# A two-layer decoder trunk: first output products split ahead of the last values' emptying, memory rows stored from GpSimd's queue, initial query slabs crosswise

## The chip, the core and the metric

The kernel runs on one core of a Trainium2 chip. Its engines work side by side, each with its own instruction stream in order: TensorE (PE) multiplies matrices from SBUF into the banks of PSUM; VectorE (DVE) and ScalarE (ACT) read PSUM and SBUF and write SBUF; GpSimd (POOL) works on SBUF alone; SyncE (SP) issues DMA transfers, and POOL's stream can issue them too. An instruction waits on semaphores for what it reads and for the buffers that it writes. The metric is device time in microseconds (us) of one execution.

## The reference

The input is x (1 x 1024 x 1024) with 256 memory tokens. Two layers, each `x <- LayerNorm(alpha * x + W_out [main * silu(g_main) ; mem * silu(g_mem)])`, with all of u_main, q_mem and the two gates from one projection `h = x @ w_in` (3072 columns).

- Layer 0's main branch is a causal pooling over windows of 2, 4, 8 and 16 tokens with a linear map per group.
- After layer 0, `x @ w_kv_shared` gives keys, values (16 heads of 64) and forget-gate logits.
- Layer 1's main branch is causal attention with a forgetting bias:

```python
logits = jnp.einsum('bqhd,bkhd->bhqk', qi, k) * scale
logits = logits + (ci[..., :, None] - cum_k[:, :, None, :])
p = jax.nn.softmax(jnp.where(mask[None, None], logits, -jnp.inf), axis=-1)
return jnp.einsum('bhqk,bkhd->bqhd', p, v)
```

- In both layers the memory branch is a 4-head attention (heads of 128) from q_mem into the 256 memory tokens, whose keys and values come from `mem @ w_mem_kv`.

## The kernel before, in words

**Numbers.** Products run at a precision near float32 with two or three matmuls for one. A tensor is held in parts: a rounded high part, a low part (the difference) and, for the three-term kind, a second rounding called top. ACT makes the high and top parts with casts, DVE the low part with a subtraction (`hi_lo`, lines 195 to 200; `scaled_hi_lo` for the two-half kind in layer 1; `gp_` variants on POOL). `three` lists the pairs of parts to be multiplied.

**Buffers.** Tiles come from pools by tag, each tag with a fixed number of buffers: "w" (6) holds split weights, "raw" (4) weights as they land, "T" (6) transposed probabilities and inputs of the output product, "V" (4) in layer 1 the memory rows and, after them, the attention's values; in PSUM "pj" (2 banks), "L" (3), "T" (2) and "O" (1). A new tile waits for the last use of the buffer that it takes.

**Order.** A planner orders each engine's instructions by their place in the program and by when it expects their inputs. Inside `with tc.manual_schedule(engines={PE})` PE keeps the program's order. `tc.keep_in_program_order(ins)` (often `pin`) keeps one instruction behind the one that was written before it for the same engine. DMA issues are instructions of SP or POOL like others, and a DMA that waits holds up what stands behind it in its queue.

**A slab** (`slab`, line 325) is one 128-column strip of a projection, over all 1024 tokens: in layer 1, for n in the two halves of the tokens and pc in the two halves of the depth, 12 matmuls of 512 columns, 48 in all. Each n has its own PSUM bank, and is emptied by the function that was passed in, right after its 24th matmul. It is a generator that yields at each matmul, so slabs can be pumped in pieces between other work.

**Layer 1's memory attention** (`mem_attention`, line 461). The norm of layer 0 (`norm`, line 668) writes the new stream X in rows of 128 tokens: normalised by DVE, split, and transposed into X by DMA (line 695). Meanwhile PE projects the four heads' memory keys (`keys`, line 419, 24 matmuls of 256 columns each, into "pj"), which need no X. Then, head by head, one query slab over X (line 470, into "pj", emptied by `q_split`, lines 457 to 459) and the head's memory values (`vals`, line 422, 24 matmuls). Here the planner orders PE too. Logits, softmax and values follow, with gate slabs between them. Last, DVE multiplies each head's rows by its gate (line 541) and SP stores them to the DRAM tensor `y1d` (line 542).

**Into the forgetting attention.** `v_first` (line 855) projects the first two pairs' values: for each of 8 token tiles 24 matmuls of 272 columns into "pj", emptied by ACT (line 872) and DVE (lines 873, 874) into two "V" buffers. `fox` (line 1150) then goes through 16 heads of 8 query tiles with the program's own order on PE, pumping projection slabs between the heads' products, `LAG` = 6 tiles ahead of the products with the values (`values`, line 1100).

**The drain.** After the last head, six more steps (hd = 16) bring the values of the last tiles. PE's filler is `OutProj.early` (line 604): the output product of layer 1 for the first 256 tokens with the third quarter of its depth, the memory rows. In the last step come the values of tiles 0 to 3 of head 15, emptied by ACT (line 1124) and DVE (1125), gated by POOL (1134) and stored by SP (1136). Then `OutProj.rest` (line 615) takes the other products in the order of line 619: (0, 0) is tokens 0 to 255 with the first third of the depth, whose rows were stored long before. It loads them (634), splits them in two halves on ACT and DVE, pinned (lines 637 to 643), and multiplies (599), then goes on with 256 tokens at a time, and normalises and stores each group.

Of the kernel before, what the change touches and what calls it, by code (L numbers as in the profile page):

```python
# [9 lines left out]
F32 = mybir.dt.float32  # L10
# [4 lines left out]
AF = mybir.ActivationFunctionType  # L15
# [3 lines left out]
P = 128  # L19
# [6 lines left out]
MH = 4  # L26
# [46 lines left out]
def run(units):  # L73
    for _ in units:
        pass
# [3 lines left out]
def trunk_kernel(ctx, tc, x, xT, memT, win, wk, wv0, wv, wmk, wmv, wout, poolw, pscale, lng, lnb, bforget, out):  # L79
# [33 lines left out]
    def T(shape=(P, S), dt=F32R):  # L113
        return sb(list(shape), "T", 6, dt)
# [338 lines left out]
    def q_split(l, to, acc):  # L453

        if not l:
            return hi_lo(to, acc)
        nc.scalar.activation(to.hi, acc, AF.Copy, scale=un1s[0])
        nc.vector.scalar_tensor_tensor(to.lo, acc, un1s[0], to.hi.bitcast(F32), ALU.mult, ALU.subtract)
        nc.scalar.activation(to.top, acc, AF.Copy, scale=un1s[0])

    def mem_attention(l, X, kv, qtile, ytile, yd, behind=None, before=None, last=None):

        (mk, v, undo), keys, vals = kv
        qs = []
        if l:
            for h in range(MH):
                keys(h)
        for h in range(MH):
            q = parts_of(qtile, [P, S])
            run(slab(win[l, 8 + h], X, lambda cols, acc: q_split(l, q[:, cols], acc)))  # L470
            qs.append(q)
            if not l:
                keys(h)
            vals(h)
        seeing[0] = None
        ys, gs = [ytile() for _ in range(MH)], [G() for _ in range(MH)]
        pt, fill = {}, Fill()
        for h in range(MH):
            fill.add(gate_units(win[l, 20 + h], gs[h], X), SLAB)
        if behind:  # L480
            fill.add(behind, 24 * NH)

        def probs(i):

            p, two = sb([P, MH, NMEM], "P", 4), sb([P, 2, MH, NMEM], "P", 4, F16)
            m, ms, sm, r = tiny(MH), tiny(MH), tiny(MH), tiny(MH)
            for hp in range(2):
                lg = ps([P, 2, NMEM], "L", 3)
                for n, j in ((0, 0), (0, 1), (1, 1), (2, 1), (1, 0), (2, 0)):
                    h = 2 * hp + j  # L490
                    a, b = three(qs[h][:, i * P : (i + 1) * P], mk[:, h, :])[n]
                    nc.tensor.matmul(lg[:, j, :], a, b, start=(n, j) == (0, 0), stop=(n, j) == (2, 0))
                pair = slice(2 * hp, 2 * hp + 2)
                nc.vector.tensor_reduce(m[:, pair], lg, AX.X, ALU.max, negate=True)
                nc.vector.tensor_scalar(ms[:, pair], m[:, pair], MSCALE, None, ALU.mult)
                for j in range(2):
                    h = 2 * hp + j
                    nc.scalar.activation(
                        p[:, h, :], lg[:, j, :], AF.Exp, bias=ms[:, h : h + 1], scale=MSCALE, accum_out=sm[:, h : h + 1],
                    )  # L500
            nc.vector.tensor_scalar(r, sm, 1.0 / PSCALE, None, ALU.mult)
            nc.vector.reciprocal(r, r)
            for h in range(MH):
                nc.scalar.activation(two[:, 0, h, :], p[:, h, :], AF.Copy, scale=r[:, h : h + 1])
                nc.vector.scalar_tensor_tensor(
                    two[:, 1, h, :], p[:, h, :], r[:, h : h + 1], two[:, 0, h, :], ALU.mult, ALU.subtract,
                )
            pt[i] = T([P, 2, MH, 2, P], F16)
            nc.sync.dma_start_transpose(
                pt[i].rearrange("p e h m q -> p (e h m) q"), two.rearrange("p e h t -> p (e h t)"),  # L510
            )

        def values(c, h):
            acc = ps([P, NH], *(("O", 1) if h == 1 else ("T", 2)))
            for j in range(4):
                t = pt[4 * c + j]
                mm3(acc[:, j * P : (j + 1) * P], [
                    (v[:, h, 2 * e + m, :], t[:, f, h, m, :])
                    for m in range(2) for e, f in ((0, 0), (0, 1), (1, 0))
                ])  # L520
            nc.vector.tensor_scalar(ys[h][:, c * NH : (c + 1) * NH], acc, undo[:, h : h + 1], None, ALU.mult)

        with tc.manual_schedule(engines={PE}):
            for t in range(ST + 2):
                part = fill.left / (ST + 2 - t)
                if t < ST:
                    probs(t)
                if before and t == ST - 2:
                    before()
                if last and t == ST:  # L530
                    last(0)
                at = {5: (0.3, 0, 0.1, 0.6), 9: (0.6, 0, 0.1, 0.3)}.get(t, (1, 0, 0, 0))
                for h in range(MH):
                    fill.pump(part * at[h])
                    if t in (5, 9):
                        values((t - 5) // 4, h)
            fill.pump(float("inf"))
        if last:
            last(1)
        for h in range(MH):  # L540
            nc.vector.tensor_tensor(ys[h], ys[h], gs[h], ALU.mult)  # L541
            nc.sync.dma_start(yd[:, h, :], ys[h])

    class OutProj:

# [2 lines left out]

        def __init__(self, l, wtile, yd):
            self.l, self.wtile, self.yd, self.ws, self.accs = l, wtile, yd, [{}, {}], None  # L550
            self.raws, self.n = [], 0

        def fetch_two(self, land):

# [49 lines left out]
        def early(self, y, ys):  # L604
# [7 lines left out]
            self.accs = self.open()  # L612
            yield from self.products(self.accs, 2, ys)

        def rest(self, resid, X, dst):
            order = [(sp, c) for sp in range(ST // 2) for c in (2, 0, 1)]
            accs, splits, gb = {}, [24], []
            if self.accs:
                accs[0], order[:6], splits = self.accs, [(0, 0), (1, 2), (0, 1), (1, 0), (1, 1)], [16, 24]
            if X is not None:  # L620
                self.split(splits.pop())

            def loads():

                for v in (lng, lnb):
                    t = sb([P, D], "P", 4)
                    nc.sync.dma_start(t, v[self.l].partition_broadcast(P))
                    gb.append(t)

            for sp, c in order:  # L630
                if c == 2:
                    accs[sp] = self.open((("T", 2), ("T", 2), ("L", 3), ("O", 1))) if 0 in accs and sp == 1 else self.open()
                src, ys = T([P, 4, 2 * P], F32), parts_of(T, [P, 4, 2 * P])
                nc.sync.dma_start(src, self.yd[c, :, :, sp * 2 * P : (sp + 1) * 2 * P])
                joins = bool(self.accs) and (sp, c) == (0, 0)
                if joins:
                    pin = tc.keep_in_program_order
                    tiles = [(ys[:, :, a * P : (a + 1) * P], src[:, :, a * P : (a + 1) * P]) for a in range(2)]
                    for to, y in tiles:
                        pin(nc.scalar.copy(to.hi, y))  # L640
                        pin(nc.vector.tensor_tensor(to.lo, y, to.hi.bitcast(F32), ALU.subtract))
                    for to, y in tiles:
                        pin(nc.scalar.copy(to.top, y))
                else:
                    hi_lo(ys, src)
                if splits:
                    self.split(splits.pop(0), X is None)
                if not gb and not splits:
                    loads()
                if c == 1:  # L650
                    zs = rows_of(resid, sp)
                run(self.products(accs[sp], c, ys, X is None and sp == ST // 2 - 1 and c == 1, joins or c > 0))
                if X is not None and (sp, c) == (0, 0):
                    scale_of_norm(gb)
                if X is not None and c == 0 and sp:
                    scales_of_weights(sp - 1)
                if X is not None and c == 0 and sp in (1, 2):
                    keep(sp - 1)
                if c == 1:
                    norm(sp, accs.pop(sp), gb, zs, X, dst)  # L660
# [152 lines left out]
    with tc.tile_pool(name="in1", bufs=1) as in1:  # L813
# [286 lines left out]
        def values(hd, c, o):  # L1100
# [20 lines left out]
                part(n == 0)  # L1121
            own, other = slice(64 * b, 64 * b + 64), slice(64 - 64 * b, P - 64 * b)
            oc = o[own, c * NH : (c + 1) * NH]
            nc.scalar.activation(oc, acc[other, :], AF.Copy, scale=un[own])  # L1124
            nc.vector.scalar_tensor_tensor(oc, acc[own, :], un[own], oc, ALU.mult, ALU.add)

        bfb = const.tile([P, HEADS], F32, name="bfb")
        nc.sync.dma_start(bfb, bforget.partition_broadcast(P))
# [21 lines left out]
        def fox(following, out_proj, head):  # L1150
# [8 lines left out]
            for hd in range(HEADS + 1):  # L1159
# [16 lines left out]
                for i in range(ST if hd < HEADS else LAG):  # L1176
# [50 lines left out]
                    fill.pump(part * FRAC[0])  # L1227
                    for what in split:
                        turn(*what)
                    older = past[0]  # L1230
                    if older and older[1] % 4 == 0:
                        values(older[0], older[1] // 4, older[2])
# [81 lines left out]
```

## Time and profile before

| what | value |
|---|---|
| three runs | 1187.91, 1190.2, 1191.57 us, median 1190.2 |
| the profiled execution | 1191.22 us, span 1189.5 us |
| granted clock of TensorE | 0.998 |
| PE, DVE, ACT, POOL busy | 98%, 66%, 58%, 24% of the span |
| HBM read, written | 116.01 MB, 22.61 MB |

The page of the profile shows one execution: the busy time of each engine; the span in 40 slices; the DMA queues; the chain of work that ended last; the costliest groups of instructions. Further views answer for one engine, tile or stretch: a timeline (start and busy time in us, engine, line, operation, what it writes and reads, how many; in brackets the idle time before it and what ended it) and waits (who waited for whom, in total, times, longest). "PEld" is the loading of weights, beside PE's matmuls, "SPq" an instruction in SP's queue. Names are the program's: `pj` is a PSUM bank, `w` a weight tile. Matmuls are pipelined and the ends of PE's rows are modelled, so the distance of starts tells more than the busy time of a short row.

### The profile page before, as it was taken

How to read it: one execution, taken by the hardware profiler on the slowest of the kernel's cores; microseconds unless marked ns; L12 is line 12 of the kernel's file. 1: busy time of each engine (PE TensorE's matmuls, PEld its weight loads, DVE VectorE, ACT ScalarE, POOL GpSimd, SP SyncE). 2: the span in 40 equal slices, each digit the busy share in tenths (PEclk: the TensorE clock that was granted, in tenths of full speed). 3: DMA queues.
4: the chain of work that ended last, by engine and by line, in shares of the span. 5: the costliest groups of instructions: out<-in, count | busy, mean ns of one | idle time of the engine just before them, and what ended most of it. 6: DMA issues, size and time to landing. Idle time of an engine off the chain costs nothing. (4 is left out here: it accounts for less than half of the span.)

```text
span 1189.5 us, 19847 instructions
## 1 busy us (share of the span) xinstructions
PE 1166.9 (98%) x6941; PEld 672.4 (57%) x6941; DVE 781.3 (66%) x1841; ACT 684.7 (58%) x1514; POOL 285.8 (24%) x437
## 2 busy tenths in 40 slices
PE   9999999999999999999999999999999999999996
PEld 5566766555555557556664555555555545455553
DVE  6744675555765557457645888778877788875554
ACT  6577875875563234467422776667766767674210
POOL 4322001310000000000002454555545444750000
PEclk9999999999999999999999999999999999999999
DMA  7575656854375555355734889989996999984430
GB/s 262 179 257 185 165 103 208 250 176 150 97 266 170 149 156 134 110 142 108 196 126 115 180 188 208 201 168 194 208 204 146 167 198 205 216 202 161 167 106 35
DMA packets 286196, 203.89 MB, mean 171 GB/s; under 512 B 224912, under 2 KB 238352, under 8 KB 286096
## 3 DMA queue, kind: packets, MB, share of 16 engines
q1 hardware_dynamic: 279696, 181.59, 61.4%
q0 software_dynamic: 6400, 21.04, 5.5%
q8 instruction: 54, 0.88, 0.3%
q14 instruction: 46, 0.38, 0.1%
HBM read 116.01 MB, written 22.61 MB: 117 GB/s over the span
## 5 line engine op out<-in xcount | busy, mean ns | idle before, releaser
L359 PE MATMUL pj<-A,w 128*128 128x512 f16 (+2 forms) x2896 | 662.3, 382 | 1.7 <-ACT w L198 0.7
L359 PEld LDWEIGHTS <-w 128*128 128x128 f16 (+1 forms) x2560 | 245.7, 98 | 278.4 <-issue 9.6
L1053 ACT ACTIVATE T<-MK,s 128x512 f32<-128x512 f32 x192 | 111.1, 579 | 66.3 <-DVE s L1045 49.4
L1082 DVE SCALAR_TENSOR_TENSOR P<-T,s,P 128x512 f16<-128x512 f32 x192 | 112.0, 613 | 39.2 <-ACT P L1081 38.1
L1081 ACT ACTIVATE P<-T,s 128x512 f16<-128x512 f32 x192 | 103.1, 576 | 53.1 <-issue 28.9
L599 PEld LDWEIGHTS <-T 128*128 128x128 bf16 x736 | 70.5, 98 | 87.9 <-issue 3.9
L1019 POOL TENSOR_SCALAR_AFFINE_SELECT raw<-R 128x256 f32<-128x256 f32 (+3 forms) x128 | 59.9, 470 | 180.7 <-DVE s L1045 97.7
L323 PE MATMUL L<-A 128*128 128x512 f16 (+3 forms) x384 | 84.7, 326 | 5.5 <-DVE s L1045 5.4
L199 DVE TENSOR_TENSOR w<-raw,w 128x512 bf16<-128x512 f32 x74 | 51.9, 701 | 54.9 <-ACT w L198 39.3
L902 POOL MEMSET G<- 128x128 f32 x1 | 0.2, 204 | 334.1 <-DVE V L541 334.1
L359 PEld LDWEIGHTS pj<-A,w 128*128 128x128 f32 x352 | 65.3, 188 | 16.2 <-ACT w L198 1.1
L199 DVE TENSOR_TENSOR T<-T,T 128x1024 bf16<-128x1024 f32 x22 | 26.8, 1220 | 65.5 <-PE pj L599 43.4
L323 PEld LDWEIGHTS <-A 128*128 128x128 f16 x384 | 37.3, 98 | 48.8 <-issue 7.6
L178 POOL TENSOR_TENSOR w<-B,w 128x512 f16<-128x512 f32 x54 | 62.9, 1166 | 4.0
L198 ACT CAST w<-raw 128x512 fp32r<-128x512 f32 x76 | 46.7, 615 | 25.0 <-DMA raw<-in_win_dram 11.2
L1107 PEld LDWEIGHTS <-V 128*64 128x64 f16 (+1 forms) x1152 | 50.6, 104 | 13.3 <-issue 5.6
L1107 PE MATMUL O<-T,V 128*64 128x128 f16 (+1 forms) x1152 | 57.5, 220 | 0.4 <-ACT T L1053 0.4
L198 ACT CAST T<-T 128x1024 fp32r<-128x1024 f32 x22 | 23.1, 1048 | 55.6 <-DMA T<-y0d 24.7
L599 PE MATMUL pj<-B,T 128*128 128x512 bf16 (+1 forms) x192 | 53.1, 385 | 0.4 <-DVE G L676 0.4
L1045 DVE CUSTOM_DVE_ANT_0 MK<-L,R,scales 128x512 f32<-128x512 f32 x64 | 45.3, 708 | 9.7 <-PE L L323 9.3
L200 ACT CAST w<-raw 128x512 bf16<-128x512 f32 x78 | 48.2, 618 | 3.3 <-PE pj L359 1.9
L599 PE MATMUL L<-B,T 128*128 128x512 bf16 (+1 forms) x168 | 47.3, 394 | 0.4 <-ACT T L640 0.4
(292 smaller groups left out, 1851.0 us busy)
## 6 DMA issues: line engine op xcount, KB each, us to landing
raw<-in_win_dram SPq DMA_DIRECT2D x66, 256.0 KB, 3.4
W<-in_win_dram POOLq DMA_DIRECT2D x48, 256.0 KB, 4.1
R<-cumd SPq DMA_DIRECT2D x16, 512.0 KB, 4.5
B<-in_win_dram SPq DMA_DIRECT2D x15, 512.0 KB, 4.8
y0d<-Y SPq DMA_DIRECT2D x12, 512.0 KB, 4.4
raw<-in_wout_dram SPq DMA_DIRECT2D x24, 256.0 KB, 2.8
T<-y0d SPq DMA_DIRECT2D x12, 512.0 KB, 4.6
A<-A SPq DMA_DIRECT2D x24, 256.0 KB, 4.0
```

Of the source, the lines that this page charges most:

```text
L178: pin(nc.gpsimd.tensor_tensor(to.lo, src, to.hi, ALU.subtract))
L198: pin(nc.scalar.copy(to.hi, src))
L199: pin(nc.vector.tensor_tensor(to.lo, src, to.hi.bitcast(F32), ALU.subtract))
L200: pin((top or nc.scalar.copy)(to.top, src))
L323: nc.tensor.matmul(acc, a, b, start=i == 0, stop=i == len(terms) - 1)
L359: nc.tensor.matmul(accs[n], a[:, k, :], b[:, pc * 4 + k, n * NH : (n + 1) * NH], start=seen[n] == 1, stop=seen[n] == 3 * KT,)
L599: nc.tensor.matmul(accs[a][nh], y, w, start=kt == 8 and i == 0, stop=kt == 7 and i == 2,)
L1019: tc.keep_in_program_order(nc.gpsimd.affine_select(C[:, :w], R[:, lo:up], [[-1, w]], ALU.is_ge, -NEG, base=w - P, channel_multiplier=1,))
L1053: nc.scalar.activation(e, p[:, lo:up], AF.Exp, bias=top, scale=-1.0, accum_out=sums[:, n, hd % 2, i : i + 1],)
L1081: nc.scalar.activation(pair[:, lo:up], e, AF.Copy, scale=r)
L1082: nc.vector.scalar_tensor_tensor(pair[:, L + lo : L + up], e, r, pair[:, lo:up], ALU.mult, ALU.subtract)
L1107: nc.tensor.matmul(acc[rows, (i % 4) * P : (i % 4) * P + P], v[:, b, 2 * j : 2 * j + (1 if e else 2), :].rearrange("p e d -> p (e d)"), pt ...
```

## The change

Three parts.

1. In layer 1's memory attention the query slabs of heads 0 and 1 are issued crosswise, with the program's order on PE: 24 matmuls (the first half of the tokens) of head 0, 24 of head 1, the rest of head 0, the values of head 0, the rest of head 1, the values of head 1. Head 0's slab takes its banks from "L" in place of "pj". Heads 2 and 3 stay as they were.
2. In layer 1 the four stores of the memory rows to `y1d` are issued from POOL's queue, pinned there, in place of SP's. Layer 0 keeps SP.
3. The load and the split of the first quarter of the output product, (0, 0), move from `rest` to a new function `begin`, which `fox` calls in the last step of the drain, ahead of the last values. The two instructions that empty these values (only those of the last head's first half) are now pinned, and so stand behind the split on ACT and DVE. The matmuls on that quarter stay in `rest`.

```diff
+        def queries(h, banks=("pj", 2)):
             q = parts_of(qtile, [P, S])
-            run(slab(win[l, 8 + h], X, lambda cols, acc: q_split(l, q[:, cols], acc)))
             qs.append(q)
+            return slab(win[l, 8 + h], X, lambda cols, acc: q_split(l, q[:, cols], acc), banks)
+
+        if l:
+            with tc.manual_schedule(engines={PE}):
+                one, two = queries(0, ("L", 3)), queries(1)
+                run(islice(one, 24))
+                run(islice(two, 24))
+                run(one)
+                vals(0)
+                run(two)
+                vals(1)
+        for h in range(2 if l else 0, MH):
+            run(queries(h))
             if not l:
                 keys(h)
             vals(h)
...
             nc.vector.tensor_tensor(ys[h], ys[h], gs[h], ALU.mult)
-            nc.sync.dma_start(yd[:, h, :], ys[h])
+            if l:
+                tc.keep_in_program_order(nc.gpsimd.dma_start(yd[:, h, :], ys[h]))
+            else:
+                nc.sync.dma_start(yd[:, h, :], ys[h])
...
+        def begin(self):
+
+            src, ys = T([P, 4, 2 * P], F32), parts_of(T, [P, 4, 2 * P])
+            nc.sync.dma_start(src, self.yd[0, :, :, : 2 * P])
+            pin, self.begun = tc.keep_in_program_order, ys
+            tiles = [(ys[:, :, a * P : (a + 1) * P], src[:, :, a * P : (a + 1) * P]) for a in range(2)]
+            for to, y in tiles:
+                pin(nc.scalar.copy(to.hi, y))
+                pin(nc.vector.tensor_tensor(to.lo, y, to.hi.bitcast(F32), ALU.subtract))
+            for to, y in tiles:
+                pin(nc.scalar.copy(to.top, y))
+
         def rest(self, resid, X, dst):
...
-                src, ys = T([P, 4, 2 * P], F32), parts_of(T, [P, 4, 2 * P])
-                nc.sync.dma_start(src, self.yd[c, :, :, sp * 2 * P : (sp + 1) * 2 * P])
+                if self.begun and (sp, c) == (0, 0):
+                    ys = self.begun
+                else:
+                    src, ys = T([P, 4, 2 * P], F32), parts_of(T, [P, 4, 2 * P])
+                    nc.sync.dma_start(src, self.yd[c, :, :, sp * 2 * P : (sp + 1) * 2 * P])
...
-            nc.scalar.activation(oc, acc[other, :], AF.Copy, scale=un[own])
-            nc.vector.scalar_tensor_tensor(oc, acc[own, :], un[own], oc, ALU.mult, ALU.add)
+            pin = tc.keep_in_program_order if (hd, c) == (HEADS - 1, 0) else lambda ins: ins
+            pin(nc.scalar.activation(oc, acc[other, :], AF.Copy, scale=un[own]))
+            pin(nc.vector.scalar_tensor_tensor(oc, acc[own, :], un[own], oc, ALU.mult, ALU.add))
...
                     for what in split:
                         turn(*what)
+                    if hd == HEADS and i == LAG - 1:
+                        out_proj.begin()
```

More of the change, by code (lines that the diff above doesn't have):

```diff
@@ L467, in mem_attention @@
                 keys(h)
-        for h in range(MH):
+        def queries(h, banks=("pj", 2)):
             q = parts_of(qtile, [P, S])
-            run(slab(win[l, 8 + h], X, lambda cols, acc: q_split(l, q[:, cols], acc)))
             qs.append(q)
+            return slab(win[l, 8 + h], X, lambda cols, acc: q_split(l, q[:, cols], acc), banks)
[10 more added lines that the diff above has]
+            run(queries(h))
             if not l:
@@ L550, in __init__ @@
             self.l, self.wtile, self.yd, self.ws, self.accs = l, wtile, yd, [{}, {}], None
-            self.raws, self.n = [], 0
+            self.raws, self.n, self.begun = [], 0, None
         def fetch_two(self, land):
@@ L632, in rest @@
                     accs[sp] = self.open((("T", 2), ("T", 2), ("L", 3), ("O", 1))) if 0 in accs and sp == 1 else self.open()
-                src, ys = T([P, 4, 2 * P], F32), parts_of(T, [P, 4, 2 * P])
-                nc.sync.dma_start(src, self.yd[c, :, :, sp * 2 * P : (sp + 1) * 2 * P])
-                joins = bool(self.accs) and (sp, c) == (0, 0)
[L636 to L644, printed above, removed]
+                if self.begun and (sp, c) == (0, 0):
[3 more added lines that the diff above has]
+                    nc.sync.dma_start(src, self.yd[c, :, :, sp * 2 * P : (sp + 1) * 2 * P])
+                joins = bool(self.accs) and (sp, c) == (0, 0)
+                if not joins:
                     hi_lo(ys, src)
```

## The prediction

> **What bounds the kernel now.** I read the page's first part, then the waits of TensorE (PE), then the timeline at each wait. First the page's span and its row for PE:
>
> ```profile
> span 1189.5 us, 19847 instructions
> ...
> PE 1166.9 (98%) x6941; PEld 672.4 (57%) x6941; DVE 781.3 (66%) x1841; ACT 684.7 (58%) x1514; POOL 285.8 (24%) x437
> ```
>
> PE is busy 98% of the span: another engine's time counts only where PE stands still for it. The waits of PE (total in us, times, longest), the two longest of the span and then those of two stretches, 460 to 500 and 1055 to 1070:
>
> ```profile
> PE L L323 <- DVE s L1045: 5.4, 7, 1.5
> PE pj L865 <- DVE G L874: 2.1, 1, 2.1
> ```
> ```profile
> PE pj L359 <- ACT MK L200: 0.6, 1, 0.6
> PE pj L359 <- DMA A<-A: 0.4, 1, 0.4
> ```
> ```profile
> PE L L599 <- ACT T L640: 0.4, 1, 0.4
> ```
>
> The first line lies in the forgetting attention, which the change leaves alone. The other four are single waits, 3.5 us together, at the three places that the change touches. So the most that it can win is four gaps, here sized by the beat of the matmuls around each, since modelled ends hide part of a gap.
>
> **Part 1: the initial slabs crosswise.** The timeline of PE at the head of layer 1's memory attention (start, busy, count, idle before), and DVE's last reading of an "L" bank before it:
>
> ```profile
> 464.96 6.72 PE L410 MATMUL pj<-T,w 128*128 128x256 f32 x56
> 472.25 6.20 PE L359 MATMUL pj<-A,w 128*128 128x512 f16 x28 [0.57 <-ACT MK L200]
> 478.86 4.48 PE L359 MATMUL pj<-A,w 128*128 128x512 f16 x20 [0.40 <-DMA A<-A]
> 482.98 3.06 PE L410 MATMUL pj<-T,w 128*128 128x256 f32 x24
> 485.88 10.52 PE L359 MATMUL pj<-A,w 128*128 128x512 f16 x48
> 496.24 2.86 PE L410 MATMUL pj<-T,w 128*128 128x256 bf16 x24
> ```
> ```profile
> 460.36 0.67 DVE L676 SCALAR_TENSOR_TENSOR G<-G,L 128x512 f32<-128x512 f32 x1
> ```
>
> 48 query matmuls take 496.24 - 485.88 = 10.36 us, 0.216 each; 24 key or value matmuls take 2.90, 0.121 each.
> - First gap. The 56 key matmuls end by the beat at 464.96 + 6.77 = 471.73; the first slab starts at 472.25, because its "pj" bank still holds a key projection. The change gives this slab the "L" banks, free since 461.0. Gain 0.52.
> - Second gap. 28 matmuls end at 472.25 + 6.05 = 478.30; the next, in the slab's second column half, starts at 478.86, when the last transposed columns of X land. Crosswise, 24 first-half matmuls of the second slab (5.2 us) come before it. Gain 0.56, with some 3 us to spare.
>
> What is late next: the weights. The second slab's must be ready 24 matmuls after 471.73, at 476.9, and take the place in the load queue of the value weights, whose loads and first casts were
>
> ```profile
> 468.86 1.90 SPq L212 DMA_DIRECT2D raw<-in_wmv_dram  x2
> ```
> ```profile
> 473.42 0.62 ACT L198 CAST w<-raw 128x512 fp32r<-128x512 f32 x1 [1.22 <-DMA raw<-in_wmv_dram]
> ```
>
> so the second slab's would land at 473.4 and, with two casts and two differences that run side by side, be split by about 476, the low parts being needed only 8 matmuls (1.7 us) into each group. In time. The value weights of head 0 now need four of the six "w" buffers while two slabs hold four: the last pair comes free only when the first slab ends, and is wanted 12 of 24 value matmuls later (1.45 us). How ScalarE (ACT) used that moment before, at the same slab's end (482.6 by the beat):
>
> ```profile
> 483.37 0.69 ACT L457 ACTIVATE B<-pj,scales 128x512 fp32r<-128x512 f32 x1 [1.82 <-PE pj L359]
> 483.96 0.71 ACT L171 ACTIVATE w<-raw,scales 128x512 f16<-128x512 f32 x1
> ```
>
> The emptying comes first, 0.7 us after the slab's end, and a cast behind it ends at 484.67, some 2.0 us after: PE would wait 0.6. If the cast goes ahead of the emptying, nothing. I take 0.2, below the middle, since three other casts of those weights are then done and ACT has been free before (1.82). Part 1: 0.52 + 0.56 - 0.2 = 0.9 gained; ends 1.1 gained, 0.9 lost (rival B).
>
> **Part 2: memory rows' stores on GpSimd's (POOL's) queue.** PE; ACT, which waits for the stores; VectorE's (DVE's) product ahead of the second; SyncE's (SP's) queue around the first; and, from the list of DMA issues, a store of the same size elsewhere:
>
> ```profile
> 593.55 6.32 PE L865 MATMUL pj<-MK,A 128*128 128x272 f16 x48
> 601.97 16.85 PE L865 MATMUL pj<-MK,A 128*128 128x272 f16 x144 [2.10 <-DVE G L874]
> 618.66 12.68 PE L359 MATMUL pj<-A,w 128*128 128x512 f16 x58
> ```
> ```profile
> 600.01 0.28 ACT L872 ACTIVATE V<-pj 128x128 f16<-128x128 f32 x1 [5.36 <-DMA y1d<-V]
> 601.17 0.45 ACT L872 ACTIVATE V<-pj 128x128 f16<-128x128 f32 x2 [0.89 <-DMA y1d<-V]
> ```
> ```profile
> 590.71 1.22 DVE L541 TENSOR_TENSOR V<-V,G 128x1024 f32<-128x1024 f32 x1
> ```
> ```profile
> 589.19 0.55 SPq L332 DMA_DIRECT2D B<-in_win_dram  x1
> 590.04 4.16 SPq L542 DMA_DIRECT2D y1d<-V  x3
> ```
> ```profile
> y1d<-R SPq DMA_DIRECT2D x3, 512.0 KB, 4.1
> ```
>
> The first values are emptied into "V" buffers that the memory rows occupy until their stores have landed: the first store lands at 600.0, 10 us after its issue, the second at 601.2. The store elsewhere takes 4.1. The difference stands ahead of it in SP's queue: four 512 KB loads, the last issued at 589.19. 144 matmuls take 618.66 - 601.97 = 16.69, 0.116 each, so 48 should take 5.56, to 599.11; PE resumes at 601.97, 2.86 late. Not all of that is the store: the first 48 are busy 6.32 us in place of 5.56, and with 0.2 off for the modelled end of the last, 0.56 is a pause for weights inside the group, which stays. Gain up to 2.3.
>
> What the stores cost on POOL's queue is bounded by layer 0's loads there (min/median/max in ns), and by POOL's first wait behind the new place:
>
> ```profile
> L258 POOL DMA_DIRECT2D W<-in_win_dram x48: 546/546/736, 24.4 to 229.8; - x48
> ...
> DMA to landing us min/median/max: 2.8/3.9/7.0
> ```
> ```profile
> 621.60 0.62 POOL L193 TENSOR_SCALAR w<-B 128x512 f16<-128x512 f32 x1 [27.18 <-PE pj L359]
> ```
>
> Four issues at 0.55 us are 2.2 us of POOL; each waits there for its product (the second's ends at 591.93), and so does the scaling of the gate's weights traced behind them. That stays hidden: POOL stood idle for 27 us after it, waiting for PE till 621.6. The landing of 256 KB took 2.8 to 7.0 us on that queue, so for 512 KB I take 4 to 8 after an issue that ends at 592.5: the second store lands between 596.5 and 600.5. PE needs it by 598.9 to go on at 599.7. I take 597.5, nearest to the median 3.9 plus the longer transfer: no wait is left and the gain is 2.3. PE followed the second landing by 0.8 (601.17 to 601.97), so at 600.5 the gain is 0.7, and at the present 9 us from issue it is nothing. SP loses four issues, behind which PE awaited nothing; its loads now share the engines with the stores, and PE's waits name none of them.
>
> **Part 3: the output product's first quarter split ahead.** PE and ACT in the drain; SP's load of the quarter, with its landing; and PE's first matmul on the second quarter:
>
> ```profile
> 1061.73 0.59 PE L599 MATMUL pj<-B,B 128*128 128x512 bf16 x2
> 1062.77 0.73 PE L599 MATMUL L<-B,T 128*128 128x512 f32 x2 [0.45 <-ACT T L640]
> ```
> ```profile
> 1061.40 0.68 ACT L1124 ACTIVATE G<-O,scales 64x512 f32<-64x512 f32 x1 [5.35 <-PE O L1107]
> 1062.10 1.14 ACT L640 CAST T<-T 128x512 fp32r<-128x512 f32 x2
> ```
> ```profile
> 1054.81 1.44 SPq L634 DMA_DIRECT2D T<-y1d  x2
> ```
> ```profile
> DMA to landing us min/median/max: 6.3/6.3/6.3
> ```
> ```profile
> 1083.96 0.81 PE L599 MATMUL L<-R,T 128*128 128x512 f32 x2
> ```
>
> Two matmuls take 0.43, so PE should go on at 1062.16 and goes on at 1062.77: 0.6 lost, because the cast L640 stands behind the last values' emptying L1124. The load lands at 1054.8 + 6.3 = 1061.1. Ahead of the emptying, the first cast ends at 1061.1 + 0.62 = 1061.8: no wait, with 0.4 in hand. Gain 0.6; if the load slips by half a microsecond, 0.4. The price: the emptying waits behind four casts (two of 1.14 together, and two more of the same size), to about 1063.4, 2.0 late, and with it its DVE step, POOL's gating, the store of the last pair, and the load of the second quarter behind that store. That quarter enters PE at 1083.96; from the late store at about 1067.4 it needs a store's and a load's landing (4.1 and at most 6.3) and a cast of 1.1: 1079. Free, with 5 us in hand.
>
> **Sum.** 0.9 + 2.3 + 0.6 = 3.8 us, nearly all of it PE time with PE-bound work behind it, so it reaches the end. On the profiled execution: 1191.2 (span 1189.5) to 1187.4, span 1185.7. That execution was 1.0 above the median 1190.2, so for the median 1186.4, 0.32% less. A measurement of this kernel can tell about 0.3% (3.6 us): the forecast lies just past that edge, 1186.6.
>
> **Rivals.**
> - A: the stores land no sooner. The last numbers of this window's row (share of the 16 DMA engines, GB/s; before them the busy times, DVE's the third) show them full:
>
> ```profile
> 590.00:592.00 2.00, 2.00 (x26) 1.41 (x24) 1.97 (x4) 0.00 (x0) 0.00 (x0) 1.00 1.02 346
> ```
>
> The bytes ahead are the same, so another queue may only move the issue. Against it: the row of 4.1 for the same size. Gain of part 2 then nothing, total 1.5: 1188.7. The Trainium skill (DMA: Bandwidth & Descriptors, Issuing engines are not separate DMA queues) states this: spreading issues only saves issue time. The same page (Queues, rings and completion order) says that each engine goes round between queue rows by packet, by which a store on an empty row does not stand behind the loads; no run yet shows which holds here.
> - B: crosswise weights stall the values. If buffers are handed out in turn, head 1's first value pair also waits for the second slab's end, another cast, 0.5 to 1.4 us in front of PE; with up to 0.6 at head 0, part 1 ends between 0.4 gained (1.1 - 0.2 - 0.5) and, at 1.4 and 0.6, 0.9 lost. At the latter the total is 2.0: 1188.2. For it: six buffers against eight wanted. Against it: head 0's four buffers come free 24 matmuls (5.2 us) earlier and would be taken first.
> - C, the other side: POOL's issues are held up by DVE. DVE is full just then (1.97 of 2 us above), with products of two operands (1.22 us each). Place: the second store's landing. It makes the kernel slower by over 0.3% when it lands 3.6 + 1.5 (the other two parts' gain) = 5 us after the present 601.2, at 606, which is 14 us from its product: 1194. Against it: 48 issues of 546 ns, none over 736, in a layer where DVE worked too. The Trainium skill (SBUF — State Buffer, A bandwidth-pool intuition that's wrong (but worth ruling out)) has such a rule: GpSimd cannot write descriptors while DVE holds their shared port, which made 3.1 us of 0.62 beside a DVE copy; by that, an estimate, the second issue would end near 596.2, its store land near 601, and part 2 gain nothing.
> - D: the planner orders ACT, DVE and SP otherwise in the forgetting attention, whose seven waits are 5.4 us: about 1 us either way.
>
> **Chances.** Forecast 0.70, A 0.10, B 0.07, C 0.09, D alone 0.04. The forecast's own range is 1185.2 to 1187.8: 0.3 either way on the gaps, and about 1 for a median of few runs. I put two thirds of it past the edge: 3.8 stands against 3.6, and what could add (no stall; a shorter pause in the first values' group) is a little more than what could take. Faster 0.70 x 2/3 + 0.02 = 0.48; slower 0.09 + 0.02 = 0.11; within 0.41. The 80% range takes in A and B with the spread of the runs shown (1187.9 to 1191.6, about 1.8 to either side): 1184.4 to 1190.4, and leaves out C.
>
> **What would show it.** PE's waits lose the lines with L874, L200, A<-A and L640. A short wait of PE at L410 behind L200 or L199 near 487 is my 0.2; one near 495 is B. The store's row shows POOL and a median landing of 4 to 7; at 9 or more A or C, C if the issues themselves take over 0.7. Wrong altogether if a new PE wait over 1 us stands in any of the three places, or if the gaps go and the span does not shrink.

## The result and the profile after

The changed kernel takes 1187.52 us (median of 14 runs, 1185.85 to 1189.1), the kernel before, beside it, 1190.63 (14 runs, 1187.04 to 1192.68). The ratio is 0.9981 with a 95% interval of 0.9974 to 0.9988, that is 2.3 us less (1.4 to 3.1). The ratio on record is not the quotient of the two medians, which is 0.9974, or 3.1 us less. By the 0.3% that a measurement of this kernel can tell, it is faster by too little to count. The forecast was 1186.4, just beyond that edge.

The page of the profiled execution after (1186.79 us), span and busy time of each engine:

```profile
span 1185.0 us, 19799 instructions
...
PE 1162.7 (98%) x6894; PEld 671.8 (57%) x6941; DVE 780.6 (66%) x1841; ACT 685.3 (58%) x1514; POOL 288.0 (24%) x441
```

PE is still the bound. The waits of PE after (who waited, for whom: total us, times, longest):

```profile
PE L L323 <- DVE s L1068: 5.6, 8, 1.5
PE idle L98 <- DVE warm L95: 1.3, 1, 1.3
PE pj L359 <- ACT A L731: 1.1, 2, 1.0
PE pj L888 <- DVE G L897: 1.0, 1, 1.0
PE L L359 <- ACT B L198: 0.6, 1, 0.6
PE pj L359 <- DVE Y L376: 0.2, 1, 0.2
PE pj L359 <- ACT w L198: 0.2, 1, 0.2
```

Of the four waits that the change was aimed at, those behind L200, A<-A and L640 are gone. The fourth, at the first values, has only halved: 2.10 at L865 before, 1.0 at L888 now. The lines for L731, L198 and L376 belong to layer 0, where the kernels are the same.

**Where the time went.** I took the same instruction of DVE and ACT in both traces and followed by how much it starts sooner after. Layer 0 is 1.06 us ahead by 460 us, though no part of the change lies there. From then on: 2.26 at 500 to 590 us, 3.35 from 600 on, still 3.36 at 1040, and 4.07 from 1140 to the end. So the three places gained 1.20, 1.09 and 0.70, together 3.0, and between these two traces the attention gained and lost nothing. PE's timeline after at the first place (start, busy, count):

```profile
463.90 6.73 PE L410 MATMUL pj<-T,w 128*128 128x256 f32 x56
470.47 5.35 PE L359 MATMUL L<-A,w 128*128 128x512 f16 x24
475.66 5.34 PE L359 MATMUL pj<-A,w 128*128 128x512 f16 x24
480.84 5.34 PE L359 MATMUL L<-A,w 128*128 128x512 f16 x24
485.83 3.12 PE L410 MATMUL pj<-T,w 128*128 128x256 f32 x24
488.79 5.34 PE L359 MATMUL pj<-A,w 128*128 128x512 f16 x24
```

The crosswise slabs run without a break. From keys to slab it is 6.57 us (7.29 before), so the first gap is worth 0.72, and the other 0.48 of the 1.20 are the second. The first values (485.83 to 488.79, 2.96) do not stall.

At the second place, PE and ACT after, then the stores on POOL and their row in the list of DMA issues (count, size, median us to landing):

```profile
591.29 6.32 PE L888 MATMUL pj<-MK,A 128*128 128x272 f16 x48
598.62 16.85 PE L888 MATMUL pj<-MK,A 128*128 128x272 f16 x144 [1.01 <-DVE G L897]
615.31 9.88 PE L359 MATMUL pj<-A,w 128*128 128x512 f16 x45
```
```profile
596.61 0.28 ACT L895 ACTIVATE V<-pj 128x128 f16<-128x128 f32 x1 [4.23 <-DMA y1d<-V]
597.82 0.45 ACT L895 ACTIVATE V<-pj 128x128 f16<-128x128 f32 x2 [0.93 <-DMA y1d<-V]
```
```profile
588.50 0.54 POOL L556 DMA_DIRECT2D y1d<-V  x1 [330.59 <-DVE V L534]
590.08 0.53 POOL L556 DMA_DIRECT2D y1d<-V  x1 [1.03 <-DVE V L554]
```
```profile
y1d<-V POOLq DMA_DIRECT2D x4, 512.0 KB, 7.6
```

The stores are on POOL, and still take 7.6 us to land (8.8 before). ACT still empties the first values behind them.

In the drain, the first matmuls on the early quarter and on the next one:

```profile
1058.62 0.81 PE L615 MATMUL L<-B,T 128*128 128x512 f32 x2
...
1079.89 0.81 PE L615 MATMUL L<-R,T 128*128 128x512 f32 x2
```

The wait of 0.45 is gone, and the second quarter enters at 1079.89 in place of 1083.96, 4.07 sooner: the late emptying cost PE nothing.

### The profile page after: what moved, and what is told of

The parts are those of the page before. It is cut to its first block, busy times and chain, and to the rows that moved or that the text cites. A ratio compares the mean times of both kernels' runs of the same rounds, so it can differ in the third digit from the quotient of the medians.

```text
span 1185.0 us, 19799 instructions
## 1 busy us (share of the span) xinstructions
PE 1162.7 (98%) x6894; PEld 671.8 (57%) x6941; DVE 780.6 (66%) x1841; ACT 685.3 (58%) x1514; POOL 288.0 (24%) x441
## 5 line engine op out<-in xcount | busy, mean ns | idle before, releaser
L359 PE MATMUL pj<-A,w 128*128 128x512 f16 (+2 forms) x2827 | 650.9, 383 | 1.7 <-DVE Y L376 0.2
L359 PEld LDWEIGHTS <-w 128*128 128x128 f16 (+1 forms) x2560 | 245.6, 98 | 277.0 <-issue 8.0
L359 PEld LDWEIGHTS pj<-A,w 128*128 128x128 f32 x352 | 65.1, 188 | 17.0 <-ACT w L198 1.5
L198 ACT CAST w<-raw 128x512 fp32r<-128x512 f32 x76 | 46.7, 615 | 23.9 <-DMA raw<-in_win_dram 8.7
L198 ACT CAST T<-T 128x1024 fp32r<-128x1024 f32 x22 | 23.1, 1048 | 59.7 <-DMA T<-y1d 30.6
L200 ACT CAST w<-raw 128x512 bf16<-128x512 f32 x78 | 48.2, 618 | 3.3 <-PE pj L359 1.9
```

Of the source, the lines that this page charges most:

```text
L198: pin(nc.scalar.copy(to.hi, src))
L200: pin((top or nc.scalar.copy)(to.top, src))
L359: nc.tensor.matmul(accs[n], a[:, k, :], b[:, pc * 4 + k, n * NH : (n + 1) * NH], start=seen[n] == 1, stop=seen[n] == 3 * KT,)
```

## The experiments

The question was why the second place gained 1.1 and not 2.3. I measure it by the 192 matmuls of the first values, from their first to the next L359 row: 618.66 - 593.55 = 25.11 us before, 615.31 - 591.29 = 24.02 after. Some expectations use a shorter stretch, the first 48 matmuls: 8.42 and 7.33.

Some of the texts on record need a correction. Those of p1_alone and p3_alone have the descriptions of their two edits exchanged; the edits as named below are what ran, and the numbers expected belong to them. And 0.57, 0.40 and 0.45, which p1_alone's and before_2's texts call waits for the stores, are the gaps of the first and third places; the wait for the stores before is the 2.10. What held_sp_timed's text calls the gate's raw loads are those of the key weights.

### The big loads held back

SP issues four 512 KB weight loads shortly ahead of the first store: 3.9 to 2.4 us ahead in the trace of the changed kernel, 2.4 to 0.9 in that of before. Here these loads, and those before them in this stretch, wait in SP's queue until the second load of the attention's key weights has gone out, behind all but the last of the stores (held_pool). In held_sp the stores are on SP again as well, all four ahead of the loads. The line that holds the loads; the lines that mark that key load are left out:

```diff
-            nc.sync.dma_start(wide, pieces_dram.rearrange("c p k m -> p c k m"))
+            with tc.issue_after(hold[-1].ins) if hold else nullcontext(): nc.sync.dma_start(wide, pieces_dram.rearrange("c p k m -> p c k m"))
```

> The changed kernel with the 512 KB weight loads for the forgetting attention held in SP's queue behind the second small load for the second pair's keys, so that none of them is under way when the memory rows are stored. Theory 1 (the stores on POOL's row get only a share of full DMA engines beside those loads): they land 4 to 5 us after their issue in place of 7.6, PE's wait of 1.01 is gone, the stretch falls from 7.33 to 6.1 to 6.4. Theory 2 (the path over POOL is slow by itself, descriptors or their start): they still land after 7 to 8 us and the stretch stays at 7.3. In both the loads come 10 us later, which I expect to cost nothing, since POOL scales the first of them long before PE asks (20 us idle).

> As the run before, the loads held back, but with the stores on SP's queue again, ahead of the loads. Theory 1: the queue of the store does not matter once nothing stands ahead: they land after about 4 us, the stretch is 6.1 to 6.3, a little less than over POOL, which starts a store 0.4 us after its product. Theory 2: they land after about 4 us here and after 7 to 8 over POOL. Theory 3 (stores to DRAM are slow in this stretch whatever else goes on): 7 us or more in both.

held_pool took 1187.64 and held_sp 1186.42, one run each, the kernel before 1189.86 beside them. PE's timeline of held_sp at the values, and the landing of its stores (tile V's view), then the same two of held_pool:

```profile
591.87 23.00 PE L888 MATMUL pj<-MK,A 128*128 128x272 f16 x192
614.71 10.52 PE L359 MATMUL pj<-A,w 128*128 128x512 f16 x48
```
```profile
DMA to landing us min/median/max: 2.6/2.6/4.6
```
```profile
593.05 23.00 PE L888 MATMUL pj<-MK,A 128*128 128x272 f16 x192
615.89 9.44 PE L359 MATMUL pj<-A,w 128*128 128x512 f16 x43
```
```profile
DMA to landing us min/median/max: 2.9/3.1/7.6
```

The 192 matmuls run without a wait: 22.84 us in both kernels, 2.27 less than before, which is all there is to gain. The stores land 2.6 us after their issue on SP, 3.1 on POOL (medians). So theory 1 holds: the big loads delay the stores, on either queue, and POOL's own path is not slow by itself. The one store that took 7.6 in held_pool is the fourth, which goes out beside the loads again, and no value waits for it. I had expected 4 to 5 for the landing; the engines are emptier than I thought.

The same stretch without the wait on the stores, by giving the values other buffers:

```diff
-            first_vs.extend(vt([P, 2, 2 * ST, 64], F16) for _ in range(2))
+            first_vs.extend(xy([P, 2, 2 * ST, 64], F16) for _ in range(2))
```

> The changed kernel with the first two pairs' values in two of the large weight buffers in place of the memory rows' buffers, so that no one waits for the stores. The planner then also issues the large loads later. All theories: the wait of 1.01 is gone and the stretch is 6.1 us, the bound for anything done to the stores. Two buffers fewer for weights until head 4 may cost up to 1 us of new waits of PE in the first heads.

1189.18 in one run; the stretch is 22.83. It is no clean test of the buffers, since these come from the ones that the big loads fill: the loads went out later, and the stores landed in 3.1 us here too. Nor does its total tell anything: its trace stands 2.35 us behind that of before already at 440 us, gains the whole 2.27 at the values, and loses nothing from there to 1000.

### Each part alone

p1_alone has the crosswise slabs alone, p2_alone the stores on POOL alone, p3_alone the early quarter alone, each put on the kernel before as the change's diff shows it.

> Only the quarter of output products moved ahead of the last values' emptying; stores on SP and the initial slabs row by row as before. My account: DVE's and ACT's instructions come 1.2 us sooner, against the stretch before 464 us, from 500 us on, nothing more at the values near 600 (store waits of 0.57, 0.40 and 0.45 as before), nothing in the drain. If part 1's 1.2 us needs another part, less; if the two new orders only pushed a wait to the values, those 1.2 us are lost again by 610 us.

> Only the initial slabs crosswise; the rest as before. My account: nothing to 1040 us, then 0.7 us in the drain (the wait of the output products for their weight rows is gone), kept to the end; emptying later by up to 2 us there without cost. If the gain in the drain comes from the other parts having moved the loads, less than 0.3.

> The kernel before with the memory rows' stores on POOL's queue alone. My theory (each part keeps its own gain, since PE is the bound between them): the stretch of PE from the first values' first matmul to the third token tile's, 8.42 us before and 7.33 with all three parts, is 7.3 here too, and the two gaps at the query slabs (0.57 and 0.40 idle) and the one in the drain (0.45) stand as before. Rival: the store's gain depends on what part 1 did to the loads ahead; then the stretch is anything between 7.0 and 8.4.

Their times were 1191.13, 1190.31 and 1189.36, one run each. At the first place p1_alone gained 1.22 (instructions 1.76 us late at 460, 0.54 at 500), in the drain p3_alone 0.72 (0.18 early at 1040, 0.90 at the end). Each is the whole gain of the changed kernel in that place, so these two parts need no other. The whole time of p1_alone shows no gain, since its layer 0 was 1.76 us late.

The miss is at the values. PE's timelines of p1_alone and of p3_alone, whose stores are on SP as before:

```profile
594.09 6.32 PE L877 MATMUL pj<-MK,A 128*128 128x272 f16 x48
601.49 16.85 PE L877 MATMUL pj<-MK,A 128*128 128x272 f16 x144 [1.07 <-DVE G L886]
```
```profile
595.08 6.32 PE L873 MATMUL pj<-MK,A 128*128 128x272 f16 x48
601.60 16.85 PE L873 MATMUL pj<-MK,A 128*128 128x272 f16 x144 [0.19 <-DVE G L882]
```

The wait was 2.10 in the trace of before, and is 1.07 and 0.19 here, with nothing changed at this place. So the 1.1 us that the changed kernel gained there cannot all be credited to the move of the stores. p2_alone, which has that move, missed its 7.3 for the first 48 matmuls and its rival's 7.0 to 8.4 as well: 6.51.

### What the second part is worth

p13 is the changed kernel with the stores on SP again; before_2, after_2 and p2_timed are the kernels before, after and p2_alone once more.

```diff
-            if l:
-                tc.keep_in_program_order(nc.gpsimd.dma_start(yd[:, h, :], ys[h]))
-            else:
-                nc.sync.dma_start(yd[:, h, :], ys[h])
+            nc.sync.dma_start(yd[:, h, :], ys[h])
```

> The changed kernel with its second part alone undone: the memory rows' stores on SP's queue as before, the quarter split and the slabs crosswise kept. If the move to GpSimd's queue is what gains at the values (the prediction's account), the matmuls of the first values wait 2.2 us again, their stretch is 8.4 us long and the median is about 1.1 us above the changed kernel's 1187.5. If it gains nothing, and what differs is how far the big loads have come when the stores begin, the stretch is 6.4 to 7.4 us as in the two looks with stores on SP and another part alone (7.40 and 6.52), and the median is within 0.5 us of 1187.5.

> The kernel before, unedited, profiled a second time. If its waits for the stores at the values (0.57, 0.40 and 0.45 us, 1.42 together, a stretch of 8.42 us and a landing of 8.8) belong to its program, they stand there again within 0.3 us. If they belong to the one execution, in which the transposing DMA just ahead of the big loads took 4.48 us of SP's time against 3.5 to 3.7 in four other traces, the stretch is 6.4 to 7.4 us, and a part of what the second part was credited with was never there to gain.

> The changed kernel once more, unedited, timed beside the next kernel. Theory 1 (the stores only get a share of DMA engines that are full with the big loads, and how much they get differs with the moment): the stores land again in 6 to 8 us and the matmuls of the first values wait 0.2 to 1.1 us for it, time 1187.0 to 1188.2. If the landing of 7.6 was one disturbed execution, it is back at 5 and the wait is gone.

> Only the memory rows' stores on GpSimd's queue, timed. The prediction's account has 2.3 us of gain here, median 1188.2. What the eight traces with the big loads ahead of the stores say by now: the values lose 0.4 to 2.3 us (five with stores on SP, mean 1.4) or 0.4 to 1.2 us (three with stores on GpSimd, mean 0.9), so the move is worth about 0.5 us, median 1189.5 to 1190.2, and the second store lands at most 6.5 us after the first values' first matmul whenever the big loads are issued.

PE's timelines of before_2 and p13:

```profile
603.61 16.85 PE L865 MATMUL pj<-MK,A 128*128 128x272 f16 x144 [1.49 <-DVE G L874]
```
```profile
599.55 16.85 PE L885 MATMUL pj<-MK,A 128*128 128x272 f16 x144 [1.25 <-DVE G L894]
```

p13's stretch of 48 is 7.57 and before_2's 7.82: both miss, lying between the two cases of their texts. The traces with the big loads ahead side by side, and two with the loads held, from PE's and SP's timelines and the landings. Times of the loads and stores are us after the first values' first matmul; "lost" is the stretch less 22.84.

| kernel | stores on | SP held by the transposing DMA ahead | last big load issued, landed | second store landed | lost |
|---|---|---|---|---|---|
| before | SP | 4.48 | -4.36, 5.04 | 7.54 | 2.27 |
| before_2 | SP | 4.23 | -4.61, 4.34 | 6.93 | 1.67 |
| p13 | SP | 4.25 | -4.60, 4.16 | 6.69 | 1.42 |
| p1_alone | SP | 3.53 | -5.32, 3.88 | 6.51 | 1.25 |
| p3_alone | SP | 3.73 | -5.10, 2.91 | 5.63 | 0.37 |
| after | POOL | 3.64 | -5.20, 5.09 | 6.45 | 1.18 |
| after_2 | POOL | 4.38 | -4.38, 7.57 | 6.47 | 1.21 |
| p2_timed | POOL | 3.91 | -4.93, 4.13 | 6.18 | 0.91 |
| p2_alone | POOL | 3.79 | -5.03, 3.46 | 5.63 | 0.36 |
| held_sp | SP | 1.86 | behind the stores | 1.02 | 0 |
| held_pool | POOL | 1.84 | behind three stores | 1.73 | 0 |

Three things are to be read in it.

- In every row with a loss it is the landing of the second store less 5.27, within 0.02. So this landing alone sets the loss here.
- On SP the second store lands 2.5 to 2.7 us after the last big load: two stores of 512 KB at 1.3 us each, behind the loads in the order of issue. How late the loads are issued hangs on the transposing DMA ahead of them in SP's queue, and that varies from one execution to the next. When they land does not follow from that alone: p1_alone's last load goes out 0.22 us earlier than p3_alone's and lands 0.97 later, and I have not found why. These two rows are from SP's timelines of before and of held_sp:

```profile
580.80 4.48 SPq L509 DMA_TRANSPOSE T<-P  x1
```
```profile
579.14 1.86 SPq L522 DMA_TRANSPOSE T<-P  x1
```

- On POOL a store need not wait for the loads. after_2's last big load goes out at 586.65 and its second store at 589.83; the lists of DMA issues for these two moments:

```profile
B<-in_win_dram SPq DMA_DIRECT2D x1, 512.0 KB, 11.9
```
```profile
y1d<-V POOLq DMA_DIRECT2D x1, 512.0 KB, 7.7
```

The load lands at 598.6, the store before it, at 597.5. The Trainium skill (DMA: Bandwidth & Descriptors, Queues, rings and completion order) says that the DMA engines go round between queue rows packet by packet; these landings agree. But the big loads are still under way, and the store gets a share of full engines only: in the trace of after the busy share of the 16 DMA engines is 0.91 to 1.07 in each stretch of about 2 us from 588 to 596.6. The traces suggest a gain only where the loads go out late: 6.47 against 7.54 for loads issued at -4.38 and -4.36, yet 5.63 against 5.63 at -5.03 and -5.10, and 6.45 against 6.51 at -5.20 and -5.32. These are three pairs of single executions.

The mean loss is 1.40 us in the five traces on SP and 0.92 in the four on POOL, a difference of 0.5 us. But the losses go from 0.37 to 2.27 on SP and from 0.36 to 1.21 on POOL, so these nine traces do not tell the half microsecond from nothing. Nor do the timed runs. p2_timed took 1189.09 against 1190.0, ratio 0.9997 (0.9988 to 1.0006): 0.4 us, not told from nothing, and its median lies below the 1189.5 to 1190.2 expected. p13 took 1188.47 against 1190.43, ratio 0.9984 (0.9975 to 0.9993): 1.9 us, the 1.2 and 0.7 of the other two parts; its median, 0.95 above the 1187.52, is nearer to the first case of its text (1.1) than to the second (within 0.5). after_2 took 1187.54 against 1190.5, ratio 0.9974 (0.9963 to 0.9985). These intervals overlap. That the second part gains anything is not shown; that it does not gain the predicted 2.3 is, since p2_timed's interval ends at 1.4 us.

### The held loads, timed

> The changed kernel with the big loads of the next phase's weights held back behind the gate's raw loads, and the four stores on SP's queue again, against before, in the same rounds as the changed kernel. One look gave 1.21 us in the first layer's end, 2.27 at the values and 0.71 in the drain, 4.2 together, against 3.0 of the changed kernel. Theory 1: 1.2 us below the changed kernel's median and 4.2 below before's, so a ratio near 0.9965; if the held loads come too late anywhere, no more than the changed kernel's 0.998.

> The version with the big loads held and the stores on SP once more, for its time alone: 1186.2 again within 0.6, below the changed kernel's 1187.5, no wait at the values, stores landing 2.6 us after their issue. If its lead came from the moment of the first measurement, 1187 or more.

held_sp came out at 1186.2 against 1190.5, ratio 0.9965 (0.9953 to 0.9977), and the second time at 1187.47 against 1190.0, ratio 0.998 (0.997 to 0.9989). It is faster than the kernel before, by 4.2 and 2.4 us. The first measurement met its expectation, the second did not, so it is not shown to be faster than the changed kernel. Its three traces have the stretch of 22.84 each time, where the changed kernel's two lose 1.2. It needs no second part: the stores stay on SP.

## Why the prediction was right or wrong

**Direction and range.** 1187.5 lies 1.1 above the forecast and inside the range of 1184.4 to 1190.4. Of the chances, "faster by over 0.3%" (0.48) did not come; "within 0.3%" (0.41) did. Of the 3.8 us predicted, the two traces show 3.0 and the ratios 2.3 and 3.1.

**Part 1, predicted 0.9: right in mechanism, 0.3 small.** Both gaps closed. The first was worth 0.72, not 0.52, since 56 key matmuls take 6.57 us and not the 6.77 by the beat that I used. The 0.2 for a stall of the values did not come: there is no wait behind L198 to L200 near 487 or 495. Rival B (head 1's values stalled) is out. The second gap varies by itself: before_2 waits 1.07 for the last transposed columns where the trace of before waited 0.40, and none of the traces with the crosswise order waits there at all.

**Part 2, predicted 2.3, measured 1.09: the term that failed.** "For 512 KB I take 4 to 8 ... I take 597.5": the store would land 5 us after the end of its issue. It landed 7.1 us after it (7.7 after its start) in both traces of the changed kernel, in the upper half of the range that I had written down and not taken, and the issue ended 0.4 later than my 592.5. Counted from the values' first matmul, as before, that is a landing at 600.0, and for this my own rule (0.7 at 600.5, and more by as much as the store is earlier) gives 1.2: the rule held, the landing was mis-sized. My durations came from 256 KB loads in layer 0 and from a store elsewhere that took 4.1; the row that showed the DMA engines full at this very moment (1.02 of them busy) I put under rival A and gave 0.10. With the loads out of the way the landing is 2.6 to 3.1: so the row of 4.1 did not show what another queue would give beside those loads. The base was too large as well: I took one execution's wait for the program's. Its loss of 2.27 is the largest of the five on SP; the others lose 0.4 to 1.7.

**Part 3, predicted 0.6: right.** It is 0.70 to 0.73 in the drain of after, after_2, p3_alone and p13. The price that I set at nothing was nothing, with the second quarter 4.07 us earlier like all else.

**The rivals.** A (the stores land no sooner, 1188.7) was nearer in cause than the forecast: with the big loads ahead the stores land late on either queue. How much too strong it is stays open: between the five traces on SP and the four on POOL lies half a microsecond, not told from nothing. The rule that it drew from the Trainium skill (DMA: Bandwidth & Descriptors, Issuing engines are not separate DMA queues) is that issues on another engine only save issue time. The trace of after_2 does not bear that out to the letter, since there the store passed a load issued 3.2 us ahead of it; for most of the wait, 0.92 of 1.40 us by the means, nothing here speaks against it. C (POOL's issues held up by DVE) did not happen: the four issues take 0.53 to 0.54 us beside a DVE that is busy for 1.97 of 2 us. The lock on the shared port that the Trainium skill (SBUF — State Buffer, A bandwidth-pool intuition that's wrong (but worth ruling out)) describes does not show in these issues. D does not show: after is 3.32 to 3.35 us ahead all through the attention, from 600 to 1000 us.

## What to carry to other kernels

A transfer that lands late beside other transfers may be late for these, and not for its queue: before it is moved to another queue, see whether the DMA engines are full at that moment, and if so try holding back those loads that nobody awaits yet, which took the whole wait away here. A wait that ends with a DMA should be looked at in more than one execution before it is entered as a gain, since what stands ahead in the queue shifts from one to the next. Gaps of an engine that wait for another engine's order, like the first and third here, came out to 0.3 us from one trace.

## What the runs showed of the hardware

- **POOL starts a DMA later than SP.** On POOL the first store begins 2.79 us ahead of the values' first matmul in all four traces, on SP 3.51 in all of those listed: 0.72 later behind the same product, and 0.38 for the others. Its issue takes 0.53 us against mostly 0.33. In held_pool, with the big loads out of the way, PE waits for neither.
- **A transposing DMA holds SP longer when loads are in flight:** 3.5 to 4.5 us with the big loads ahead, 1.83 to 1.86 without, and all that is behind it in the queue moves with it.
- **One execution's total drifts by more than this change moves.** Where nothing differs, the traces stand 1.3 us ahead to 2.4 behind that of before at 440 us, by single waits in layer 0. The attention's waits behind the row sums vary as well; of PE's waits in before_2:

```profile
PE L L323 <- DVE s L1045: 2.8, 5, 1.1
```

Before, this line has 5.4, and before_2 makes up 1.6 us between 1000 and 1060 us. I have not found what decides it.
